# A first phase that multiplies the scaled x and leaves norm and shift until the sums are read

## The chip, the cores and the metric

The kernel runs on one core of one Trainium2 chip. The metric is the device time in microseconds (us) of one execution. TensorE (PE in the profile) multiplies matrices; VectorE (DVE), ScalarE (ACT) and GpSimd (POOL) do elementwise work; SyncE (SP) issues most of the DMA transfers. Each engine works through its own list of instructions in order and waits on semaphores for the others.

## The reference

One layer of a hybrid backbone, with D = 2048 channels, 1024 latent tokens `x`, 256 context tokens `ctx`. Cut to what matters here:

```python
mod_x = silu(c) @ w_mod + b_mod               # 3 x 2048 values: shift, scale, gate
mod_c = silu(c_ctx) @ w_mod + b_mod
sh_x, sc_x, gt_x = split(mod_x, 3)
hx = rmsnorm(x, norm_g) * (1.0 + sc_x) + sh_x   # per token: x * rsqrt(mean(x*x) + eps) * norm_g
hc = rmsnorm(ctx, norm_g) * (1.0 + sc_c) + sh_c
px = split(hx @ w_in)                          # q/k, v, o, z, gates, two recurrent parts
pc = split(hc @ w_in)
# context scans of both head groups (mLSTM, RG-LRU), whose last states seed the latent scans
# latent scans, gated, concatenated to yx
x = x + gt_x * (yx @ w_out)
out = rmsnorm(x, final_g)
```

`hx @ w_in` is linear in `hx`. With r(t) the norm factor of token t, s(k) the scale of channel k and b(k) its shift, `hx[t,k] = x[t,k]*s(k)*r(t) + b(k)`, so the sum over k of `hx[t,k]*w[k,m]` equals `r(t) * sum(x[t,k]*s(k)*w[k,m]) + sum(b(k)*w[k,m])`.

## The kernel before

Channels lie on the 128 partitions, so `x` is held transposed in 16 tiles `xT[k]` of 128 channels by 1024 tokens; two neighbouring k make a pair j (8 pairs). A product in f32 is made as three products of operands split into a high and a low part: `hxh` and `hxl` for the activations, `whi` and `wlo` for the weights. Weights stream through a ring: SP loads `raw`, ACT writes `whi` (L227), DVE writes `wlo` (L228). The matmuls of a k run `whi*hxh`, `wlo*hxh`, `whi*hxl`.

**Phase A** (`phase_a`, L456 to L668). PE, DVE, ACT and SP work here in the order in which the code is written. SP first loads all 16 `xT` tiles (512 KB each), then 64 tiles `wm` of modulation weights (512 KB each, 8 per pair), with weight pieces `raw` and context tiles `cT` between them. The `wm` tiles share 32 slots (tag hx) with `xT`, `hxh` and `hxl`, and have two slots of their own; `wm_fill` issues as many loads as there are free slots. While x arrives, ACT squares it (L541), DVE adds pairs of squares (L542) and PE sums them over the channels with a matrix of ones (L544); ACT takes the root (L556) and DVE the reciprocal (L557), which gives `rxB`, the norm factor of each token on all partitions. For a pair j, `mv_group` (L504) multiplies the modulation weights, `mv_fin` transposes the result (L519) and finishes scale and shift in `ssa` (L522 to L531). `to_hx` then makes the two `hxh`/`hxl` tiles: x times scale times `rxB` on DVE (L569), plus shift on ACT (L570), the low part on DVE (L575). `main_a` (L626) runs 36 matmuls of 512 columns for each pair into six PSUM accumulators `acc`: three blocks of 128 output channels. The modulation of pair j+1 is interleaved with the products of pair j. In the last pairs the context tokens are normalised too (`ctx_pair`, L606, L607, L612).

At its end `raw_tile` (L708) copies the first two accumulators out on ACT; the two PSUM buffers that the next products need are taken until then.

**Phase B** runs the context tokens: products of the context heads (L685 to L687 and L1056 to L1058), the mLSTM gates and scans, then eight units for the recurrent part, each of which ends with a copy on ACT (L1090) and a DMA from POOL's queue (L1091). From here on a planner orders the work: a clock (`clk`) counts the time of the PE products issued so far, and small jobs (`clk.spawn`) are put into the other engines' lists when their planned time has come; a job's `yield 1.5` asks to go on 1.5 us later by that clock. `clk.until(f)` lets the planner run jobs until `f` holds, before the code that follows is written out. Temporary tiles come from pools of slots such as `CS`, nine tiles in phase B.

**`v_head0`** (L1294 to L1316) is the first product of the latent tokens after that: twice (g = 0, 1) 16 channel tiles with 12 matmuls of 272 columns each (L1302 to L1304), whose weights come from the ring in pieces of two k (128x544). It reads `hxh` and `hxl` of all 16 k. All other products of the latent tokens, the scans and the output projection follow.

The functions that the change touches:

Of the kernel before, what the change touches and what calls it, by code (L numbers as in the profile page):

```python
# [19 lines left out]
D = 2048  # L20
# [236 lines left out]
def tile_hymba(ctx: ExitStack, tc: tile.TileContext, x, x_t, ctx_t, vecs_t, w_mod_a, w_mod_g, b_mod, w_in,  # L257
# [76 lines left out]
    hch = hcs.tile([128, KT, CTX], F32R, name="hch")  # L334
    pap = lpool("pa", side="right")
# [75 lines left out]
    wm_n = {"next": 0, "keep": 5, "hx": -1}  # L411
# [6 lines left out]
    def wm_fill():  # L418

        while wm_n["next"] < 8 * KP:  # L420
            n = wm_n["next"]
            j = n // 8
            keep = wm_n["keep"] if j <= wm_n["hx"] + 1 else max(wm_n["keep"], 2)
            if live["pa"] < NWM:
                live["pa"] += 1
                t, where = pa.tile([128, 2, 512], F32, tag="wm", bufs=NWM, name=f"wm{n}"), "pa"
            elif live["hx"] < NHX - keep:
                t, where = hx_tile([128, 2, 512], F32, f"wm{n}"), "hx"
            else:
                return  # L430
# [3 lines left out]
            if n == 8:  # L434
                ring._dma()
            if n == 23:
# [19 lines left out]
    def phase_a():  # L456
# [4 lines left out]
        for k in range(KT):  # L461
            xT[k] = hx_tile([128, SEQ], F32, f"xT{k}")
            SP.dma_start(out=xT[k], in_=x_t[k])
        ring._dma()
        wm_n["keep"] = 4
        wm_fill()
        silP = pa.tile([128, KT, 32], F32, name="silP")
        POOL.memset(silP, 0.0)
        act(out=cc[:, 1, :], in_=silc, func=AF.Sigmoid)
        act(out=cc[:, 2, :], in_=cc[:, 0, :], func=AF.Sigmoid)  # L470
        DVE.tensor_tensor(out=silc, in0=silc, in1=cc[:, 1, :], op=MUL)
        DVE.tensor_tensor(out=silP[:, :, 1], in0=cc[:, 0, :], in1=cc[:, 2, :], op=MUL)
        DVE.tensor_copy(out=silP[:, :, 0], in_=silc)
# [19 lines left out]
        def mv_group(j, g):  # L493
# [19 lines left out]
        def mv_fin(j):  # L513
# [20 lines left out]
        nacc = [mx_tile() for _ in range(2)]  # L534
        rxt = pa.tile([128, 2, SEQ], F32, tag="xp", bufs=1, name="rxt")
        rxB, vt = rxt[:, 0, :], rxt[:, 1, :]
        for j in range(KP):
            sq = []
            for u in range(2):
                sq.append(hx_tile([128, SEQ], F32, f"sq{2 * j + u}"))  # L540
                act(out=sq[u], in_=xT[2 * j + u], func=AF.Square)  # L541
            DVE.tensor_tensor(out=sq[0], in0=sq[0], in1=sq[1], op=ADD)  # L542
            for hf in range(2):
                PE.matmul(out=nacc[hf], lhsT=ones, rhs=sq[0][:, 512 * hf:512 * hf + 512], start=(j == 0), stop=(j == KP - 1))  # L544
            del sq
            live["hx"] -= 2
        wm_n["keep"] = 0
        wm_fill()
        for g in range(4):
            mv_group(0, g)  # L550
            if g == 1:
                for _ in range(2):
                    ring._split()
                for hf in range(2):
                    o = rxB[:, 512 * hf:512 * hf + 512]
                    act(out=o, in_=nacc[hf], func=AF.Sqrt, scale=1.0 / D, bias=eps)  # L556
                    DVE.reciprocal(out=o, in_=o)  # L557
        nacc.clear()

        def to_hx(j):  # L560
# [19 lines left out]
            if g == 1:  # L580
# [1042 lines left out]
```

## Time and profile before

| | |
|---|---|
| median of 3 runs | 1865.52 us (1865.25 to 1867.12) |
| profiled execution | 1863.79 us, its span 1862.0 us |
| mean granted clock of TensorE | 0.996 of full speed |
| PE busy | 1801.4 us, 97% of the span |
| DVE busy | 898.1 us, 48% |
| ACT busy | 772.2 us, 41% |
| POOL busy | 284.8 us, 15% |

The span is the time between the first and the last instruction that the profile records, and the 1.8 us between it and the execution's own time lie around it. The shares are means over the whole span; a stage in which PE waits for another engine is found by cutting the span into stretches.

### The profile page before, as it was taken

How to read it: one execution, taken by the hardware profiler on the slowest of the kernel's cores; microseconds unless marked ns; L12 is line 12 of the kernel's file. 1: busy time of each engine (PE TensorE's matmuls, PEld its weight loads, DVE VectorE, ACT ScalarE, POOL GpSimd, SP SyncE). 2: the span in 40 equal slices, each digit the busy share in tenths (PEclk: the TensorE clock that was granted, in tenths of full speed). 3: DMA queues.
4: the chain of work that ended last, by engine and by line, in shares of the span. 5: the costliest groups of instructions: out<-in, count | busy, mean ns of one | idle time of the engine just before them, and what ended most of it. 6: DMA issues, size and time to landing. Idle time of an engine off the chain costs nothing.

```text
span 1862.0 us, 24089 instructions
## 1 busy us (share of the span) xinstructions
PE 1801.4 (97%) x9114; PEld 1478.5 (79%) x9114; DVE 898.1 (48%) x1625; ACT 772.2 (41%) x1190; POOL 284.8 (15%) x382
## 2 busy tenths in 40 slices
PE   6998999999999999999999999999999999999998
PEld 2557999788897878987798878777888877888786
DVE  5576553436434664255443443655555454334432
ACT  5446542346645522133312422576555542223322
POOL 0000010012001210012000210222212332222320
PEclk9999999999999999999999999999999999999999
DMA  9974674212132334224342214122222584436533
GB/s 383 398 261 149 172 201 112 68 48 73 57 98 56 106 101 131 73 78 106 101 132 84 61 45 137 28 91 67 64 71 71 191 288 155 135 125 238 168 120 119
DMA packets 229444, 240.22 MB, mean 129 GB/s; under 512 B 25904, under 2 KB 184768, under 8 KB 229328
## 3 DMA queue, kind: packets, MB, share of 16 engines
q1 hardware_dynamic: 219360, 207.03, 36.5%
q0 software_dynamic: 4704, 16.78, 2.5%
q10 hardware_dynamic: 5264, 14.88, 2.0%
q8 instruction: 71, 1.16, 0.2%
q14 instruction: 45, 0.37, 0.1%
HBM read 210.78 MB, written 27.87 MB: 128 GB/s over the span
## 4 chain that ended last, share of the span: by engine, by line
PE 75%; DMA 9%; DVE 6%; issue 4%; ACT 4%; POOL 1%; SPq 0%; ACTq 0%; DVEq 0%; POOLq 0%
PE mm L1288 12%; PE mm L1285 12%; PE mm L1282 12%; PE mm L1325 2%; PE mm L1327 2%; PE mm L1328 2%; DMA wm<-in_w_mod_a_dram 2%; DMA raw<-in_w_out_dram 2%; PE mm L1470 2%; PE mx L1469 2%; PE mx L1471 2%; PE mx L1470 2%; PE mm L1471 2%; PE mm L1469 2%; DVE wlo L228 1%
## 5 line engine op out<-in xcount | busy, mean ns | idle before, releaser
L228 DVE TENSOR_TENSOR wlo<-raw,whi 128x512 fp32r<-128x512 f32 (+2 forms) x396 | 289.7, 741 | 577.1 <-ACT whi L227 576.1
L227 ACT ACTIVATE whi<-raw 128x512 fp32r<-128x512 f32 (+2 forms) x396 | 242.9, 624 | 563.8 <-PE mm L1285 249.3
L1282 PE MATMUL mm<-hxh,whi 128*128 128x512 f32 x1184 | 385.2, 406 | 0.3 <-DVE Gx L1314 0.3
L1288 PE MATMUL mm<-hxh,wlo 128*128 128x512 f32 x1184 | 373.2, 396 | 0.0
L1285 PE MATMUL mm<-hxl,whi 128*128 128x512 f32 x1184 | 372.7, 395 | 0.0
L1285 PEld LDWEIGHTS mm<-hxl,whi 128*128 128x128 f32 x1184 | 222.9, 188 | 52.9
L1288 PEld LDWEIGHTS mm<-hxh,wlo 128*128 128x128 f32 x1184 | 223.1, 188 | 51.7
L1282 PEld LDWEIGHTS mm<-hxh,whi 128*128 128x128 f32 x1184 | 221.2, 189 | 49.3 <-ACT s L1312 0.5
L1325 PE MATMUL mm<-whi,hxh 128*128 128x256 f32 x384 | 110.1, 287 | 0.3 <-DVE s L1363 0.2
L1327 PE MATMUL mm<-wlo,hxh 128*128 128x256 f32 x384 | 108.1, 281 | 0.0
L1328 PE MATMUL mm<-whi,hxl 128*128 128x256 f32 x384 | 107.4, 281 | 0.0
L1470 PE MATMUL mm<-wlo,hxh 128*128 128x512 f32 x224 | 88.7, 396 | 4.6 <-DVE wlo L228 4.6
L1469 PE MATMUL mm<-whi,hxh 128*128 128x512 f32 x224 | 88.3, 394 | 0.8 <-ACT whi L227 0.8
L1469 PE MATMUL mx<-whi,hxh 128*128 128x512 f32 x224 | 88.4, 395 | 0.0
L1471 PE MATMUL mx<-whi,hxl 128*128 128x512 f32 x224 | 88.1, 393 | 0.0
L1470 PE MATMUL mx<-wlo,hxh 128*128 128x512 f32 x224 | 88.1, 393 | 0.0
L1471 PE MATMUL mm<-whi,hxl 128*128 128x512 f32 x224 | 88.0, 393 | 0.0
L1039 DVE SCALAR_TENSOR_TENSOR r<-r,cols,r 128x256 f32<-128x256 f32 x120 | 60.1, 500 | 37.3 <-DMA r<-in_w_mod_g_dram 35.4
L1325 PEld LDWEIGHTS mm<-whi,hxh 128*128 128x128 f32 x384 | 72.4, 189 | 1.1 <-PE mx L1262 0.6
L1327 PEld LDWEIGHTS mm<-wlo,hxh 128*128 128x128 f32 x384 | 72.4, 188 | 0.3
L1328 PEld LDWEIGHTS mm<-whi,hxl 128*128 128x128 f32 x384 | 72.2, 189 | 0.0
L1507 POOL TENSOR_TENSOR res<-res,xpc 128x512 f32<-128x512 f32 x28 | 39.7, 1438 | 211.4 <-DMA raw<-in_w_out_dram 131.8
(324 smaller groups left out, 3055.1 us busy)
## 6 DMA issues: line engine op xcount, KB each, us to landing
raw<-in_w_in_dram SPq DMA_DIRECT2D x134, 512.0 KB
wm<-in_w_mod_a_dram SPq DMA_DIRECT2D x64, 512.0 KB
raw<-in_w_out_dram SPq DMA_DIRECT2D x64, 512.0 KB
r<-in_w_mod_g_dram SPq DMA_DIRECT2D x128, 128.0 KB
xT<-in_x_t_dram SPq DMA_DIRECT2D x16, 512.0 KB
NI<-niD SPq DMA_DIRECT2D x64, 128.0 KB
xpc<-in_x_dram SPq DMA_DIRECT2D x32, 256.0 KB
yD<-s ACTq DMA_DIRECT2D x15, 512.0 KB
```

The lines of the kernel that those rows point to most:

```text
L227: self.nc.scalar.activation(out=hi, in_=src, func=AF.Copy)
L228: self.nc.vector.tensor_tensor(out=lo, in0=src, in1=hi.bitcast(F32), op=SUB)
L1039: DVE.scalar_tensor_tensor(out=a, in0=t, scalar=silc[:, k:k + 1], in1=a, op0=MUL, op1=ADD)
L1282: PE.matmul(out=ps[:, ts], lhsT=hi, rhs=hxh[k][:, ts], start=(k == 0), stop=False)
L1285: PE.matmul(out=ps[:, ts], lhsT=hi, rhs=hxl[k][:, ts], start=False, stop=False)
L1288: PE.matmul(out=ps[:, ts], lhsT=lo, rhs=hxh[k][:, ts], start=False, stop=(k == KT - 1))
L1325: PE.matmul(out=o, lhsT=hxh[k][:, sl], rhs=hi, start=(k == 0 and tt % 2 == 0), stop=False, skip_group_check=True)
L1327: PE.matmul(out=o, lhsT=hxh[k][:, sl], rhs=lo, start=False, stop=False, skip_group_check=True)
L1328: PE.matmul(out=o, lhsT=hxl[k][:, sl], rhs=hi, start=False, stop=(k == KT - 1), skip_group_check=True)
L1469: PE.matmul(out=pst[jt], lhsT=hxh[j][:, sl], rhs=hi, start=(j == 0), stop=False)
L1470: PE.matmul(out=pst[jt], lhsT=hxh[j][:, sl], rhs=lo, start=False, stop=False)
L1471: PE.matmul(out=pst[jt], lhsT=hxl[j][:, sl], rhs=hi, start=False, stop=(j == KT - 1))
```

## The change

Phase A multiplies `x*scale` alone. The norm factor and the shift no longer stand in its operands, and so `x` need not all be there before the first product. The parts:

- SP loads eight `wm` tiles first, then `xT` two tiles at a time between the groups of eight `wm`, so that x and modulation weights of a pair arrive together. The rule for free slots in `wm_fill` is new; the last `xT` tile takes one of the two `wm` slots.
- `to_ux` takes the place of `to_hx`: ACT writes `hxh` straight from `xT` (Copy with scale, L569), ACT squares `xT` (L571, L573), POOL adds the square into `rxB` (L574, 128x1024, for 15 of the 16 k), DVE writes `hxl` (L577). The squares of all k but the first pass through one tile, `vt`.
- `x_norm` (L582 to L592), two matmuls with ones, two roots and two reciprocals, stands between the products of the last two k.
- `shift_sum` (L594 to L596): 32 DVE instructions of 128x384 sum the weights times shift into `wacc`; PE sums `wacc` over the channels at the end, DVE copies the result to `wb` (L695).
- `raw_tile` and `gate_tile` multiply the accumulators by `rxB` as they read them and add `wb`.
- Since later products need the full `hx`, a job `to_h` turns the tiles over in phase B: 64 blocks of 128x256, four for each k, each with two instructions on POOL (L875, L876), one on ACT (L878) and one on DVE (L879). The code waits for its end before `v_head0`.

```diff
 def wm_fill():
         while wm_n["next"] < 8 * KP:
             n = wm_n["next"]
             j = n // 8
-            keep = wm_n["keep"] if j <= wm_n["hx"] + 1 else max(wm_n["keep"], 2)
+            ahead = j - 1 - wm_n["hx"]
+            free = NHX - live["hx"] - (2 * ahead + 1 if ahead > 0 else 0)
+            if j and wm_n["x"] <= 2 * j + 1:
...
+                x_load()
+                continue
             if live["pa"] < NWM:
...
-            elif live["hx"] < NHX - keep:
+            elif free >= 1:
...
-            if n == 8:
+            if n == 7:
                 ring._dma()
+                x_load()
+                x_load()
...
+        wacc = pa.tile([128, 384], F32, name="wacc")
...
-        def to_hx(j):
+        def to_ux(j):
             for k in (2 * j, 2 * j + 1):
-                sh = ssa[:, k, 2:3]
+                sx = ssa[:, k, 0:1]
                 for ts in hs:
-                    DVE.scalar_tensor_tensor(out=vt[:, ts], in0=xT[k][:, ts], scalar=ssa[:, k, 0:1], in1=rxB[:, ts], op0=MUL, op1=MUL)
-                    act(out=hxh[k][:, ts], in_=vt[:, ts], func=AF.Identity, bias=sh)
+                    act(out=hxh[k][:, ts], in_=xT[k][:, ts], func=AF.Copy, scale=sx)
+                if k == 0:
+                    act(out=rxB, in_=xT[k], func=AF.Square)
+                else:
+                    act(out=vt, in_=xT[k], func=AF.Square)
+                    POOL.tensor_tensor(out=rxB, in0=rxB, in1=vt, op=ADD)
                 for ts in hs:
-                    DVE.scalar_tensor_tensor(out=hxl[k][:, ts], in0=vt[:, ts], scalar=sh, in1=hxh[k][:, ts].bitcast(F32),
-                                             op0=ADD, op1=SUB)
+                    DVE.scalar_tensor_tensor(out=hxl[k][:, ts], in0=xT[k][:, ts], scalar=sx, in1=hxh[k][:, ts].bitcast(F32),
+                                             op0=MUL, op1=SUB)
...
+        def x_norm():
+            ps = [mx_tile() for _ in range(2)]
+            for hf in range(2):
+                PE.matmul(out=ps[hf], lhsT=ones, rhs=rxB[:, 512 * hf:512 * hf + 512], start=True, stop=True)
+            for hf in range(2):
+                o = rxB[:, 512 * hf:512 * hf + 512]
+                act(out=o, in_=ps[hf], func=AF.Sqrt, scale=1.0 / D, bias=eps)
+                DVE.reciprocal(out=o, in_=o)
+
+        def shift_sum(k, w):
+            DVE.scalar_tensor_tensor(out=wacc, in0=w.bitcast(F32), scalar=ssa[:, k, 2:3], in1=wacc, op0=MUL, op1=ADD)
...
         def raw_tile(n, m):
             for hf in range(2):
-                act(out=j2r(st)[:, halves[hf], :], in_=jv(acc[m][hf]), func=AF.Copy)
+                DVE.tensor_tensor(out=j2r(st)[:, halves[hf], :], in0=jv(acc[m][hf]), in1=jv(rxB[:, 512 * hf:512 * hf + 512]), op=MUL)
             acc[m] = None
+            act(out=st, in_=st, func=AF.Identity, bias=wb[m])
...
+    def to_h():
+        for k in range(KT):
+            sh = b1sc[:, k:k + 1]
+            for q in range(4):
+                ts = slice(256 * q, 256 * q + 256)
+                hi = hxh[k][:, ts].bitcast(F32)
+                v = yield from CS.get()
+                v = v[:, 0:256]
+                POOL.tensor_tensor(out=v, in0=hi, in1=hxl[k][:, ts].bitcast(F32), op=ADD)
+                POOL.tensor_tensor(out=v, in0=v, in1=rxB[:, ts], op=MUL)
+                yield 1.5
+                act(out=hxh[k][:, ts], in_=v, func=AF.Identity, bias=sh)
+                DVE.scalar_tensor_tensor(out=hxl[k][:, ts], in0=v, scalar=sh, in1=hi, op0=ADD, op1=SUB)
+                CS.free()
+                yield 1.2
+        cflag["h"] = True
...
+    clk.spawn(to_h(), 10.0, P['hx'])
...
+    clk.until(lambda: "h" in cflag)
     for h in range(NH):
         if h == 0:
             v_head0()
```

Three places in the lists of the engines follow. The first is the end of phase A on DVE, from the modulation of the last pair to the first split of context weights behind it. Before:

```order
L569 SCALAR_TENSOR_TENSOR rxt<-xT_148,ssa,rxt 128x512 x2
L575 SCALAR_TENSOR_TENSOR hxl_1125<-rxt,ssa,hxh_1120 128x512 x2
L569 SCALAR_TENSOR_TENSOR rxt<-xT_150,ssa,rxt 128x512 x2
L575 SCALAR_TENSOR_TENSOR hxl_1133<-rxt,ssa,hxh_1128 128x512 x2
L228 TENSOR_TENSOR wlo_1154<-raw_1037,whi_1153 128x544
L606 SCALAR_TENSOR_TENSOR rxt<-cT_389,ssa,rcB 128x256 x2
L612 SCALAR_TENSOR_TENSOR hcl_1173<-rxt,ssa,hch 128x256 x2
L606 SCALAR_TENSOR_TENSOR rxt<-cT_391,ssa,rcB 128x256 x2
L612 SCALAR_TENSOR_TENSOR hcl_1186<-rxt,ssa,hch 128x256 x2
L228 TENSOR_TENSOR wlo_1190<-raw_1037,whi_1189 128x544
```

The changed kernel, from the low parts of the last pair (`hxl`) on; `vt` at L623 is the context scratch, which has the name of the squares' tile:

```order
L577 SCALAR_TENSOR_TENSOR hxl_1099<-xT_948,ssa,hxh_1094 128x512 x2
L577 SCALAR_TENSOR_TENSOR hxl_1107<-xT_950,ssa,hxh_1102 128x512 x2
L596 SCALAR_TENSOR_TENSOR wacc<-whi_940,ssa,wacc 128x384
L596 SCALAR_TENSOR_TENSOR wacc<-wlo_941,ssa,wacc 128x384
L228 TENSOR_TENSOR wlo_1130<-raw_1006,whi_1129 128x544
L596 SCALAR_TENSOR_TENSOR wacc<-whi_1009,ssa,wacc 128x384
L623 SCALAR_TENSOR_TENSOR vt<-cT_341,ssa,rcB 128x256 x2
L629 SCALAR_TENSOR_TENSOR hcl_1150<-vt,ssa,hch 128x256 x2
L596 SCALAR_TENSOR_TENSOR wacc<-wlo_1010,ssa,wacc 128x384
L623 SCALAR_TENSOR_TENSOR vt<-cT_343,ssa,rcB 128x256 x2
L629 SCALAR_TENSOR_TENSOR hcl_1164<-vt,ssa,hch 128x256 x2
L592 RECIPROCAL rxB<-rxB 128x512 x2
```

The two reciprocals of the norm and part of the shift sums now stand in this list behind the context pairs; two more shift sums, the copy of `wb` and the two reads of accumulators at L739 follow behind them.

The second place is POOL around the last DMA of the recurrent units (`xrcD`). Before:

```order
L1091 DMA xrcD<-c_2862 128x256
L1315 MEMSET s_3109 128x4
L811 MEMSET gxms 64x8
L995 MEMSET cwb 128x512
L745 MEMSET r_3807 128x1
L746 MEMSET r_3807 128x2
L739 TENSOR_SCALAR r_3861<-r_3807,cols 128x256
```

The changed kernel, from the last two such DMAs on:

```order
L1144 DMA xrcD<-c_2915 128x256
L875 TENSOR_TENSOR c_2999<-hxh_603,hxl_608 128x256
L875 TENSOR_TENSOR c_3004<-hxh_611,hxl_616 128x256
L1144 DMA xrcD<-c_2996 128x256
L876 TENSOR_TENSOR c_2999<-c_2999,rxB 128x256
L876 TENSOR_TENSOR c_3004<-c_3004,rxB 128x256
L875 TENSOR_TENSOR c_3009<-hxh_611,hxl_616 128x256
L875 TENSOR_TENSOR c_3014<-hxh_611,hxl_616 128x256
L876 TENSOR_TENSOR c_3009<-c_3009,rxB 128x256
L876 TENSOR_TENSOR c_3014<-c_3014,rxB 128x256
```

Behind the last `xrcD` stand the second instructions of two blocks of `to_h` (`c_2999`, `c_3004`) and then both instructions of 35 more blocks: 72 instructions of 128x256, from the last block of one k (`hxh_603`, which is k = 6) through k = 15.

The third place is ACT around the weight pieces of `v_head0` (L227, 128x544, two k each). Before, behind the copy of the last recurrent unit:

```order
L1090 ACTIVATE c_2862<-mm_2791 128x256
L227 ACTIVATE whi_2895<-raw_2773 128x544
L227 ACTIVATE whi_2926<-raw_2812 128x544
L227 ACTIVATE whi_2954<-raw_2812 128x544
L227 ACTIVATE whi_2985<-raw_2847 128x544
L227 ACTIVATE whi_3013<-raw_2847 128x544
```

The changed kernel, at the end of `to_h`; `hxh_1102` is the tile of k = 15:

```order
L878 ACTIVATE hxh_1094<-c_3159,b1sc 128x256
L878 ACTIVATE hxh_1102<-c_3164,b1sc 128x256
L878 ACTIVATE hxh_1102<-c_3169,b1sc 128x256
L878 ACTIVATE hxh_1102<-c_3174,b1sc 128x256
L878 ACTIVATE hxh_1102<-c_3179,b1sc 128x256
L227 ACTIVATE whi_3273<-raw_2941 128x544
L227 ACTIVATE whi_3304<-raw_2979 128x544
L227 ACTIVATE whi_3332<-raw_2979 128x544
```

The piece for k = 10 and 11 (`whi_3273`) now stands behind the last block of `to_h`, the piece for k = 8 and 9 behind the third block of k = 12, and the piece for k = 6 and 7 behind the third block of k = 7; DVE has its low parts in the same places.

## Rows read from the trace of the kernel before

**Rows 1.** Busy time by stretch: stretch, its length, engines with counts, PEclk, DMA, GB/s

```profile
0.00:41.27 41.27, 26.11 (x77) 9.05 (x77) 23.84 (x48) 24.38 (x29) 2.44 (x12) 1.00 0.98 380
41.27:138.40 97.13, 95.32 (x489) 51.62 (x490) 64.86 (x135) 39.19 (x68) 0.00 (x0) 1.00 0.91 334
138.40:150.50 12.10, 10.86 (x47) 8.46 (x45) 10.31 (x19) 7.50 (x12) 0.00 (x0) 1.00 0.13 35
150.50:283.00 132.50, 126.45 (x1010) 123.12 (x1011) 73.75 (x152) 70.46 (x122) 8.24 (x28) 1.00 0.67 187
283.00:307.70 24.70, 24.38 (x195) 24.06 (x193) 7.89 (x16) 6.43 (x11) 3.27 (x11) 1.00 0.48 122
307.70:1862.00 1554.30, 1518.25 (x7300) 1262.16 (x7300) 717.50 (x1259) 624.23 (x949) 270.83 (x331) 1.00 0.35 105
```

**Rows 2.** Chain of waits, first 165 us: start, length, what

```profile
6.86 9.81 DMA xT<-in_x_t_dram
...
78.40 0.44 PE mx L519 x4
...
91.92 0.44 PE mx L519 x4
...
112.92 6.92 DMA wm<-in_w_mod_a_dram
...
127.61 4.78 DMA wm<-in_w_mod_a_dram
...
150.50 0.39 PE mm L685
```

**Rows 3.** Groups by line, first 150 us: busy us, mean ns of one

```profile
L570 ACT ACTIVATE hxh<-rxt,ssa 128x512 fp32r<-128x512 f32 x32 | 22.2, 724 | 30.5 <-DVE rxt L569 28.0 <-DMA raw<-in_w_in_dram 2.4
L541 ACT ACTIVATE sq<-xT 128x1024 f32<-128x1024 f32 x16 | 15.8, 1046 | 2.5 <-PE mx L544 2.3 <-DVE sq L542 0.2
L228 DVE TENSOR_TENSOR wlo<-raw,whi 128x384 fp32r<-128x384 f32 x16 | 8.8, 554 | 14.9 <-ACT whi L227 14.9
L606 DVE SCALAR_TENSOR_TENSOR rxt<-cT,ssa,rcB 128x256 f32<-128x256 f32 x16 | 7.0, 479 | 0.0
L557 DVE RECIPROCAL rxt<-rxt 128x512 f32<-128x512 f32 x2 | 6.6, 3322 | 1.2 <-ACT rxt L556 1.2
L708 ACT ACTIVATE stx<-mm 128x512 f32<-128x512 f32 x2 | 1.9, 1048 | 0.0
```

**Rows 4.** POOL's groups by line and shape, whole span

```profile
L936 POOL TENSOR_TENSOR s<-s,s 128x1024 f32<-128x1024 f32 x16 | 38.5, 2405 | 125.6 <-ACT s L934 125.6
...
L1188 POOL TENSOR_TENSOR QI<-s,NI 128x128 f32<-128x128 f32 x64 | 33.2, 519 | 23.0 <-DVE s L1136 22.9
...
L968 POOL TENSOR_TENSOR s<-s,s 128x1024 f32<-128x1024 f32 x8 | 25.2, 3153 | 111.7 <-DVE s L958 111.7
L936 POOL TENSOR_TENSOR r<-r,r 128x256 f32<-128x256 f32 x16 | 11.9, 746 | 80.0 <-ACT r L934 65.7 <-DVE wlo L228 11.4 <-DMA raw<-in_w_in_dram 2.9
```

**Rows 5.** Timeline at 405 us: start, length, engine, line

```profile
405.42 0.69 DVE L228 TENSOR_TENSOR wlo<-raw,whi 128x512 fp32r<-128x512 f32 x1 [0.17 <-ACT whi L227]
...
405.56 0.86 POOL L1184 TENSOR_TENSOR D<-NI,msk 128x128 f32<-128x128 f32 x1 [5.03 <-DMA NI<-niD]
...
406.39 0.46 POOL L1188 TENSOR_TENSOR QI<-s,NI 128x128 f32<-128x128 f32 x1
```

**Rows 6.** Timeline at POOL's last unit DMA

```profile
284.32 0.54 POOL L1091 DMA_DIRECT2D xrcD<-c  x1 [5.19 <-ACT c L1090]
```

**Rows 7.** Timeline of ACT behind the last unit's copy

```profile
286.39 0.66 ACT L227 ACTIVATE whi<-raw 128x544 fp32r<-128x544 f32 x1 [2.36 <-PE mm L1304]
289.40 0.66 ACT L227 ACTIVATE whi<-raw 128x544 fp32r<-128x544 f32 x1 [2.35 <-PE mm L1304]
```

**Rows 8.** Timeline of PE at both ends of `v_head0`'s first half

```profile
283.01 0.29 PE L1302 MATMUL mm<-whi,hxh 128*128 128x272 f32 x1
...
307.08 0.29 PE L1304 MATMUL mm<-whi,hxl 128*128 128x272 f32 x1
```

**Rows 9.** Busy time by stretch where the granted clock falls, columns as before

```profile
350.00:354.00 4.00, 4.00 (x13) 2.94 (x14) 1.06 (x1) 1.16 (x2) 0.00 (x0) 0.57 0.10 13
```

More of the change, by code (lines that the diff above doesn't have):

```diff
@@ L334, in tile_hymba @@
     hch = hcs.tile([128, KT, CTX], F32R, name="hch")
+    rxB = hcs.tile([128, SEQ], F32, name="rxB")
     pap = lpool("pa", side="right")
@@ L410, in tile_hymba @@
     wm_t = {}
-    wm_n = {"next": 0, "keep": 5, "hx": -1}
+    wm_n = {"next": 0, "x": 0, "hx": -1}
     def hx_tile(shape, dtype, name):
@@ L433, in wm_fill, with x_load @@
             wm_t[n] = (t, where)
[L434 removed]
+            if n == 7:
                 ring._dma()
[L436 removed]
+                x_load()
+                x_load()
+            if n == 15:
+                ring._dma()
+            if n == 31:
                 for jc in range(KP):
                     load_ctx(jc)
+    def x_load():
+        k = wm_n["x"]
+        wm_n["x"] += 1
+        if k == KT - 1:
+            live["pa"] += 1
+            xT[k] = pa.tile([128, SEQ], F32, tag="wm", bufs=NWM, name=f"xT{k}")
+        else:
+            xT[k] = hx_tile([128, SEQ], F32, f"xT{k}")
+        SP.dma_start(out=xT[k], in_=x_t[k])
     def load_ctx(j):
@@ L460, in phase_a @@
         ncp = [hx_tile([128, SEQ], F32, "ncp")]
[L461 to L465, printed above, removed]
         wm_fill()
-        silP = pa.tile([128, KT, 32], F32, name="silP")
+        silP = pa.tile([128, 2 * KT + 32], F32, name="silP")
+        silV = silP[:, 0:2 * KT].rearrange("p (k s) -> p k s", s=2)
+        wacc = pa.tile([128, 384], F32, name="wacc")
         POOL.memset(silP, 0.0)
+        POOL.memset(wacc, 0.0)
         act(out=cc[:, 1, :], in_=silc, func=AF.Sigmoid)
@@ L531, in mv_fin @@
             DVE.tensor_tensor(out=ssa[:, ks, 2:4], in0=ssa[:, ks, 2:4], in1=two(cols[:, cSH + 2 * j:cSH + 2 * j + 2]), op=ADD)
[L534 to L548, printed above, removed]
+            DVE.tensor_copy(out=b1sc[:, ks], in_=ssa[:, ks, 2])
+        vt = pa.tile([128, SEQ], F32, tag="xp", bufs=1, name="vt")
         for g in range(4):
@@ L553, in phase_a @@
                     ring._split()
[L554 to L558, printed above, removed]
-        def to_hx(j):
+        def to_ux(j):
             if j >= KP:
@@ L603, in ctx_pair @@
             ks = (2 * j, 2 * j + 1)
-            fv = [vt[:, CTX * u:CTX * u + CTX] for u in range(2)]
+            o = 2 * CTX * (j % 2)
+            fv = [(ncp[0] if ncp else vt)[:, o + CTX * u:o + CTX * u + CTX] for u in range(2)]
             for k in ks:
@@ L660, in phase_a @@
                         ctx_norm(4 * j - 5)
+                    if j == KP - 2:
+                        ncp.clear()
+                        live["hx"] -= 1
                     mv_fin(j + 1)
-                    to_hx(j + 1)
+                    to_ux(j + 1)
+                    for w in (hi, lo):
+                        shift_sum(k, w[:, 0, :])
                     some(15)
-            if j == 4:
-                ncp.clear()
-                live["hx"] -= 1
-                wm_fill()
+        ps = mx_tile()
+        for m in range(3):
+            PE.matmul(out=ps[:, 4 * m:4 * m + 4], lhsT=wacc[:, cs_of[m]], rhs=ones[:, 0:4], start=True, stop=True)
+        wb = pa.tile([128, 12], F32, name="wb")
+        DVE.tensor_copy(out=wb, in_=ps[:, 0:12])
+        acc.append([wb[:, 4 * m:4 * m + 1] for m in range(3)])
         return acc
@@ L713, in gate_tile @@
             if hf == 0:
-                acc.append(pa.tile([128, 2, SEQ], F32, tag="xp", bufs=1, name="stz"))
-            stz = acc[3]
-            sg = stz[:, 0, 512 * hf:512 * hf + 512]
-            act(out=sg, in_=acc[1][hf], func=AF.Sigmoid)
-            DVE.tensor_tensor(out=j2r(stz[:, 1, :])[:, halves[hf], :], in0=jv(acc[1][hf]), in1=jv(sg), op=MUL)
+                acc.append(pa.tile([128, SEQ], F32, tag="xp", bufs=1, name="stg"))
+                acc.append(pa.tile([128, SEQ], F32, tag="wm", bufs=NWM, name="stz"))
+            stg, stz = acc[3:5]
+            zt, sg = stg[:, 0:512], stg[:, 512:1024]
+            DVE.tensor_tensor(out=zt, in0=acc[1][hf], in1=rxB[:, 512 * hf:512 * hf + 512], op=MUL)
+            act(out=sg, in_=zt, func=AF.Sigmoid, bias=wb[1])
+            DVE.scalar_tensor_tensor(out=j2r(stz)[:, halves[hf], :], in0=jv(zt), scalar=wb[1], in1=jv(sg), op0=ADD, op1=MUL)
             if hf:
-                ACT.dma_start(out=pre[1], in_=stz[:, 1, :])
+                ACT.dma_start(out=pre[1], in_=stz)
                 acc[1] = None
```

22 lines of the change are left out of this document (14 added, 8 removed).

## The prediction

> **What bounds the kernel now.** I read the page first: PE is busy for 97% of the span, so a gain can only come from a stretch in which PE has little to do, and a loss from any stretch in which the change makes PE wait. Cutting the span by stage [rows 1] shows where. Up to 41.27 us PE is busy for 26.11 us with the norm's sums and the first modulation weights, and the first real product starts at its end; DMA moves 380 GB/s there. Up to 138.40 PE is busy for 95.32 of 97.13 us. The next stretch, to 150.50, is the end of phase A, and from there to 283.00 the context runs. The first half of `v_head0` takes 283.01 to about 307.1, the start and near the end of it [rows 8]; behind it PE has 1518 of 1554 us.
>
> Then the chain of waits [rows 2]. It begins with DMA (x until 16.7), then follows PE pair by pair: the transposes of successive pairs stand at 78.40 and 91.92, 13.5 us apart, the 36 matmuls of one pair and the modulation work of the next. For the last pairs a `wm` transfer is in the chain again, 6.92 and 4.78 us from issue to landing, because a slot has to come free first. The context's first product is at 150.50, 12.1 us behind the ready scale of the last pair (138.40).
>
> **The change in phase A.** *The start.* The first product then needs eight `wm`, one weight piece, four x tiles and two more `wm` of the next pair: about 15 transfers of 0.52 MB, 7.9 MB, which at 380 GB/s [rows 1] take 20.7 us after the first 2 us, so products start near 23 instead of 41.3: 18 us earlier. What follows is no longer PE's pace. A pair now needs 8 `wm`, 2 x and a piece, 5.8 MB, 15 us at 380 GB/s, against 13.5 us of PE [rows 2]; so DMA sets the pace and the lead shrinks to about 10 us at the last pair but one.
>
> *The last pair.* I expect most of the lead lost here. By the lists, the loads of x15 and of the last pair's `wm` wait for slots: `wm` 58 for the matmul of 57, 61 for that of 59, 63 for that of 61. With the landing times of the two `wm` transfers in the chain (4.78 and 6.92 us [rows 2]) and about 1 us of matmuls behind each, three such steps make 18 to 24 us behind the first quarter (near 114); with the transposes and the scale behind them I take 135 for the ready scale, against 138.4. Its bounds: 126 if the stream stays unbroken (80 transfers of 0.52 MB and some 6 MB of pieces and context, 48 MB at 380 GB/s), 139 if the loads come late throughout.
>
> *The tail.* Before, the context starts 12.1 us behind the scale. Now the norm hangs on the last x tile's square, and the squares pass through one tile, `vt`. Behind the scale stand, each waiting for the one before: two `hxh` halves on ACT (2 x 0.72) and a square (1.05) [rows 3], an add of 128x1024 on POOL (2.41 [rows 4]), the last square (1.05; it may not write `vt` before the add has read it), the last add (2.41): 8.4 us. Beside the adds DVE makes low parts from two inputs in SBUF, for which I add 1.7 us (below), and some 0.9 us for the hand-overs: 11.0. Only now is `vt` free for the context pairs' scratch: eight DVE instructions at 0.48 [rows 3], 3.8 us; the root (0.2 us not hidden); two reciprocals at 3.32, 6.6; one split of 0.7; two shift sums of 128x384 at 0.55, 1.1; the sum of `wacc` and its copy, 1.2 (two engine hand-overs); two reads of accumulators at the 1.05 us that ACT needs for a half [rows 3], 2.1. Together 15.7, so the context starts 26.7 us behind the scale. At 135 + 26.7 = 161.7 it is **11.2 us** later than 150.50. Before, the same reciprocals lay under the wait for `wm`. Bounds: 126 + 25 = 151 to 139 + 28 = 167, or 0 to +16.5.
>
> PE has little to do for the 20 us ahead of that point. The stretch at 350 us [rows 9] has a granted clock of 0.57, near the lower level (1.2 GHz), for 4 us, with PE busy throughout: a loss of 4 x 0.43 = 1.7 us. I add **1.7** for each long stop of PE. In that row the fall comes without an idle stretch ahead of it, so it carries the price and not the cause. The Trainium skill (TensorE: Matmul & The Clock Gate, Part 1: The HAM clock gate) says that an idle array falls back to 1.2 GHz and is given the full clock again only after working for a while; by that both stops pay once, and without it the sum is 3.4 us less. No row here shows a fall after idling.
>
> **The change in phase B.** `to_h` issues 64 x 2 POOL, 64 ACT and 64 DVE instructions. Those on ACT and DVE lie in the context stage, where each has some 60 us free of 132.5 [rows 1]; I put them at nothing there, with 0 to 6 us as the bound if they delay weight splits. POOL decides. Its list holds the `xrcD` DMAs between the blocks, and each waits for the copy of its recurrent unit: the last one issues at 284.32, for 0.54 [rows 6], behind a wait of 5.19 us, so POOL does not run past that point before it. With T0 = 283.01 the start of `v_head0` [rows 8], POOL is free at T0 + 1.85. The order shows 72 of its instructions still behind. The nearest row is the same shape and operation kind, 128x256 at 0.746 [rows 4]: 72 x 0.746 = 53.7 us.
>
> Beside them runs DVE's L879, two inputs in SBUF. The timeline at 405 us [rows 5] shows what this does: a 128x128 instruction on POOL takes 0.86 us while DVE's two-input split (0.69) overlaps 0.55 of it, and the next, alone, 0.46; so 0.40 is lost in 0.55 of overlap, about 75%. One L879 per block at 0.48 (L606 is the same form [rows 3]) costs POOL 0.36, 36 times 13.0 us. The Trainium skill (GPSIMD Engine Reference, 8. Key points) has the rule: GpSimd shares its SBUF interfaces with VectorE and is hindered by DVE instructions with two SBUF inputs. The trace agrees by these two durations. Taking the row without the rule, as an accident of this one place, `to_h` would end 13 us earlier, which is a rival below.
>
> POOL ends at T0 + 1.85 + 53.7 + 13.0 = T0 + 68.6. Then L878 on ACT (0.45), and behind it the weight piece for k = 10, 11: split on ACT 0.66 [rows 7], low part 0.7; PE goes on at T0 + 70.4. PE has done k = 0 to 9 by then: up to k = 7 unhindered at T0 + 12, k = 8 and 9 once the piece behind the third block of k = 12 is through, some 45 us behind T0. Three pieces are left, 3.0 us each by the distance of successive pieces [rows 7], 9.0, and 1.7 for the clock: T0 + 81.1, against T0 + 24.1. That is **57.0 us** lost. Nothing gives it back, since everything that follows needs this output or PE, which had 2% free there. Of the stop itself weight loads profit, but PE did not wait for these.
>
> Bounds for POOL's part: 128x1024 at 2.41 is 0.60 for each 256 columns, and 128x128 at 0.46 alone [rows 4, 5]: a 128x256 can hardly be under 0.6, 72 x 0.6 = 43.2, less 10.5; from L968, 3.15 for 128x1024, 0.79 a quarter and 0.15 for the start, 0.94, 72 x 0.94 = 67.7, more 14.
>
> **Sum.** 11.2 + 1.7 + 57.0 = 69.9 us. Against the profiled execution of 1863.8 (span 1862.0 and 1.8 around it) it gives 1933.7; the median lies 1.7 higher, 1865.5, and gives 1935.4. I say **1935**.
>
> **The rivals.**
> 1. *No contention.* POOL holds 0.746 beside DVE. The tail is 1.7 shorter, `to_h` 13: 1935 - 15 = 1920. For it: 0.746 is a mean over instructions that ran beside DVE's ordinary work already. Against: the row at 405 us.
> 2. *POOL slower still*, by the rate of L968 (0.94), or DVE's other instructions hindering it too: 1935 + 14 = 1949.
> 3. *`to_h` hidden, the tail shows.* If POOL did a block within the 24 us of the first half, only phase A and one clock term count: 1865.5 + 11.2 + 1.7, about 1878. It needs 36 blocks in 24 us, 0.33 us an instruction; POOL takes 0.46 for half the columns. Against it speak all of POOL's rows.
> 4. *The other side.* The DMA stream stays unbroken: x arrives with its weights, nothing waits for a slot, and the last scale is ready at 126, 12 us before now. The price of the tail, 14.6 us more than now, is then nearly paid, and the waits of the early context stage for weights shrink (6 of 132.5 us are idle [rows 1]): 126 + 25 = 151, less up to 6, so 145 to 151 against 150.5. If `to_h` is hidden as in rival 3, the time is 1860 to 1866. The point from which it decides is the same 0.33 us on POOL; with POOL as its rows show, an unbroken stream alone gives 1925.
>
> **How the numbers follow.** 0.2% is 3.7 us; differences below it can't be told from no change here. My forecast with its own spread (1926 to 1943) has 0.50; rival 1 0.22, rival 2 0.13, rival 3 0.07, rival 4 0.05, anything else 0.03. Adding both phase A bounds (-11, +5) to the outer values of rivals 1 and 2 gives 1909 to 1954; beyond it on the lower side lie rivals 3 and 4 (0.12), so the range of 8 in 10 is 1898 to 1955. Faster: 0.03 of rival 4. Same: 0.02. Slower: 0.95.
>
> **What would show it.** In the profile after: first product of phase A near 23 us (start); a `wm` transfer as the chain's cause in the last pair, scale at 126 to 139; the two reciprocals behind the adds of POOL and ahead of the first context product near 162 (tail); POOL without a pause behind its last `xrcD`, 66 to 70 us long, its 128x256 instructions alternating between about 0.75 and 1.1 (contention); PE idle twice in `v_head0`, at k = 8 and k = 10, ended by a weight split whose engine was held by `to_h`. The forecast is wrong if POOL's blocks lie well ahead of `v_head0` in time, if its instructions take under 0.5 us, or if PE finds other work during the stop.

## The result, and the profile after

The changed kernel takes 1955.92 us (median of 4 runs, 1954.85 to 1957.21), against 1865.38 for the kernel before on the same chip: a ratio of 1.048, interval 1.0465 to 1.0495. The forecast was 1935 with a range to 1955; the direction holds, and the measured time lies 0.9 us beyond the upper end. The profiled execution took 1956.38 us, its span 1954.6.

The span cut at the marks that answer to [rows 1] (columns as there: stretch, its length, engines with counts, PEclk, DMA, GB/s): first product, last pair's scale, first context product, `v_head0`, its second half.

```profile
0.00:24.90 24.90, 11.58 (x44) 2.17 (x44) 8.71 (x39) 9.08 (x14) 4.37 (x14) 0.85 0.95 365
24.90:147.30 122.40, 105.00 (x494) 56.60 (x493) 82.69 (x138) 49.92 (x80) 31.58 (x13) 0.91 0.86 322
147.30:174.11 26.81, 15.62 (x57) 11.37 (x55) 23.06 (x26) 8.69 (x15) 5.16 (x2) 0.81 0.08 21
174.11:325.90 151.79, 137.41 (x1011) 132.01 (x1012) 112.04 (x183) 81.17 (x149) 56.60 (x84) 0.93 0.57 160
325.90:399.39 73.49, 32.52 (x195) 30.88 (x193) 40.46 (x52) 24.69 (x48) 60.87 (x83) 0.67 0.16 41
399.39:1954.60 1555.21, 1519.49 (x7300) 1262.92 (x7300) 717.94 (x1261) 624.42 (x949) 272.80 (x331) 1.00 0.35 105
```

Against [rows 1]: the context starts 23.6 us later (174.11 for 150.50), its stage is 19.3 longer (151.8 for 132.5), the first half of `v_head0` 48.8 longer (73.5 for 24.7), the rest 0.9. Together 92.6, which is the difference of the spans (1954.6 less 1862.0). The stage in which I had put the conversion at nothing (bound 6) took a fifth of the loss.

The groups of DVE in the first 174 us (busy us, mean ns of one) show the first sign of why.

```profile
L577 DVE SCALAR_TENSOR_TENSOR hxl<-xT,ssa,hxh 128x512 fp32r<-128x512 f32 x32 | 34.0, 1101 | 10.3 <-ACT hxh L569 10.3
L596 DVE SCALAR_TENSOR_TENSOR wacc<-wlo,ssa,wacc 128x384 f32<-128x384 f32 x16 | 23.8, 1488 | 0.4
L596 DVE SCALAR_TENSOR_TENSOR wacc<-whi,ssa,wacc 128x384 f32<-128x384 f32 x16 | 9.7, 604 | 0.0
```

Two shift sums of the same shape and form differ by a factor of 2.5: the one that falls beside POOL's add takes 1488 ns, the other 604. The extreme case stands behind the last `xrcD`. DVE's timeline there, then POOL's (start, length, engine, line):

```profile
326.66 0.73 DVE L228 TENSOR_TENSOR wlo<-raw,whi 128x544 fp32r<-128x544 f32 x1 [0.71 <-ACT whi L227]
329.11 10.82 DVE L879 SCALAR_TENSOR_TENSOR hxl<-c,b1sc,hxh 128x256 fp32r<-128x256 f32 x4 [1.72 <-ACT hxh L878]
```

```profile
327.77 1.44 POOL L876 TENSOR_TENSOR c<-c,rxB 128x256 f32<-128x256 f32 x2
329.17 1.43 POOL L875 TENSOR_TENSOR c<-hxh,hxl 128x256 f32<-128x256 f32 x2
...
336.12 1.40 POOL L876 TENSOR_TENSOR c<-c,rxB 128x256 f32<-128x256 f32 x2
337.88 1.76 POOL L875 TENSOR_TENSOR c<-hxh,hxl 128x256 f32<-128x256 f32 x2 [0.36 <-DVE hxl L879]
```

POOL runs at 0.70 us an instruction, as if alone, while DVE's first L879 (0.48 alone) does not get through: it begins at 329.11 and ends only when POOL itself pauses, at 337.5, for want of a `CS` tile that this very instruction still reads. The chain of waits gives this one instruction 8.71 us.

The theory for the experiments: POOL and DVE share a path into SBUF that one of them holds for a whole instruction; a DVE instruction with two inputs in SBUF waits for it, and POOL's back-to-back instructions pass it on to each other. The first half agrees with the Trainium skill (SBUF — State Buffer, Who interferes with whom), which calls the shared port pair an exclusive lock, held for the whole instruction, that a two-input DVE instruction contends for with GpSimd's reads. That POOL's next instruction takes the lock ahead of the DVE instruction that waits is read from the rows above alone. The rivals: proportional slowing, as in the prediction; slots and transfers in phase A; the added work itself.

### The profile page after: what moved, and what is told of

It reads as the page before. It is cut to its first block, busy times and chain, and to the rows that moved or that the text cites. A ratio compares the mean times of both kernels' runs of the same rounds, so it can differ in the third digit from the quotient of the medians.

```text
span 1954.6 us, 24332 instructions
## 1 busy us (share of the span) xinstructions
PE 1821.6 (93%) x9092; PEld 1495.9 (77%) x9092; DVE 984.9 (50%) x1696; ACT 798.0 (41%) x1252; POOL 431.4 (22%) x526
## 4 chain that ended last, share of the span: by engine, by line
PE 67%; DVE 10%; DMA 10%; ACT 5%; issue 4%; POOL 4%; SPq 0%; ACTq 0%; DVEq 0%; POOLq 0%
PE mm L1341 11%; PE mm L1338 11%; PE mm L1335 11%; DMA wm<-in_w_mod_a_dram 3%; DVE wlo L228 3%; DMA raw<-in_w_out_dram 3%; PE mm L1378 2%; PE mm L1380 2%; PE mm L1381 2%; PE mm L1524 2%; PE mx L1523 2%; PE mx L1525 2%; PE mx L1524 2%; PE mm L1525 2%; PE mm L1523 2%
## 5 line engine op out<-in xcount | busy, mean ns | idle before, releaser
L228 DVE TENSOR_TENSOR wlo<-raw,whi 128x512 fp32r<-128x512 f32 (+2 forms) x396 | 301.0, 772 | 566.1 <-ACT whi L227 559.5
L227 ACT ACTIVATE whi<-raw 128x512 fp32r<-128x512 f32 (+2 forms) x396 | 242.5, 624 | 577.1 <-PE mm L1338 246.4
L1237 POOL TENSOR_TENSOR D<-NI,msk 128x128 f32<-128x128 f32 x64 | 31.5, 491 | 215.3 <-DMA NI<-niD 131.2
```

Of the source, the lines that this page charges most:

```text
L227: self.nc.scalar.activation(out=hi, in_=src, func=AF.Copy)
L228: self.nc.vector.tensor_tensor(out=lo, in0=src, in1=hi.bitcast(F32), op=SUB)
```

## Experiments

The tables of stages below come from the profiled execution of each kernel, at the same marks: start of the context, its stage, first half of `v_head0`.

### Without to_h

```diff
-    clk.spawn(to_h(), 10.0, P['hx'])
-    clk.until(lambda: "h" in cflag)
```

> The job to_h and the wait for it are left out (the latent products then run on x times scale, so the output is not the layer's). Theory (the shared path between POOL and DVE is held by one of them for a whole instruction, and POOL's back-to-back adds and products in to_h keep DVE's two-input splits out): phase A stays as in the changed kernel (context starts near 174, +23.6), the context stage falls back from 151.8 to 133-137 us, the first half of v_head0 from 72.4 to 24-25; time 1890 to 1895. Rival (the context stage is longer because it starts with a low clock and late weights): it stays near 148-152 us, time 1905 to 1910.

Measured: 172.7, 137.4, 24.6; 1895.5 us, ratio 1.0141 (1.0118 to 1.0164). The theory's numbers, stage and time 0.4 and 0.5 us over their upper ends. So 14.4 us of the context stage's 19.3 come from `to_h`. The other 4.9 go with a clock of 0.96 in place of 1.00: PE's matmuls are busy for 130.76 us where [rows 1] have 126.45, 4.3 more, and 0.6 is idle time. The row of this run:

```profile
172.70:310.10 137.40, 130.76 (x1011) 127.31 (x1012) 76.97 (x156) 71.08 (x122) 8.08 (x28) 0.96 0.62 177
```

### Without to_h and without POOL's adds

```diff
-                    POOL.tensor_tensor(out=rxB, in0=rxB, in1=vt, op=ADD)
```

> As the run without to_h, and the 15 POOL adds of squares are left out too (the norm is then that of one channel tile). Theory (POOL's adds lock DVE's low parts and shift sums out, 15 us of DVE time in phase A, and the norm waits for the last add): the scale of the last pair is ready at 138-142 instead of 147, the tail behind it is 22-23 instead of 26.8, the context starts at 160-165. Rival (transfers and slots alone set the pace of phase A): the scale stays at 146-148, only the tail is shorter, context at 169-171.

Measured: the last transpose starts at 139.9 for 144.6 in the run above, the context starts at 164.5 for 172.7; 1884.96 us, ratio 1.0083 (1.0066 to 1.01). The low parts and the shift sums have their short lengths again (a line is gone, so L577 and L596 are L576 and L595 here):

```profile
L576 DVE SCALAR_TENSOR_TENSOR hxl<-xT,ssa,hxh 128x512 fp32r<-128x512 f32 x32 | 22.6, 749 | 10.3 <-ACT hxh L569 10.3
L595 DVE SCALAR_TENSOR_TENSOR wacc<-wlo,ssa,wacc 128x384 f32<-128x384 f32 x16 | 9.9, 616 | 0.4
```

The adds cost 4.7 us ahead of the scale and 3.5 in the tail. But the scale is still not early: the transposes of the last pair but one come at 115.5 and the last ones 24 us later, so the adds are 4.7 of the 12 us by which I missed the scale. Since the run takes away the adds themselves, it does not separate their lock on DVE from ACT's wait for `vt`, except in the tail, where the chain below runs through the held DVE instructions.

### to_h without its DVE instruction

```diff
-                DVE.scalar_tensor_tensor(out=hxl[k][:, ts], in0=v, scalar=sh, in1=hi, op0=ADD, op1=SUB)
```

> to_h without its DVE instruction (the low parts stay those of x times scale). Theory of the exclusive path: POOL runs without a stop at 0.70 us an instruction, 72 of them 50.4 us, so the first half of v_head0 takes 64-65 instead of 72.4; the weight splits are still kept out by POOL, so the context stage stays well above 132.5, at 142-150. Rival (DVE and POOL slow each other in proportion to the overlap, L879 being the disturber): context back at 133-136, v_head0 at 66-68.

Measured: 173.5, 146.7, 68.1; 1948.06 us, ratio 1.0414 (1.0394 to 1.0434). The context stage went as the theory had it (the rival's 133 to 136 is out), `v_head0` did not, its 68.1 lies by the rival's 66 to 68: I had left out that the weight splits are two-input instructions as well. DVE's timeline, then PE's:

```profile
327.43 45.02 DVE L228 TENSOR_TENSOR wlo<-raw,whi 128x544 fp32r<-128x544 f32 x2 [5.71 <-ACT whi L227]
```

```profile
371.33 0.59 PE L1355 MATMUL mm<-wlo,hxh 128*128 128x272 f32 x1 [41.66 <-DVE wlo L228]
```

Two splits of 0.72 us take 45.0 us, while POOL runs from 322.1 to 371.8 without a pause; PE stands for 41.7 us. L879 was not the disturber but another victim, and by blocking POOL through the tile it reads it had even opened a gap in which DVE got on. Most of the 41.7 us PE would have lost without the lock as well, since ACT splits the piece for k = 10 and 11 only behind the last block of `to_h`, as the lists above have it:

```profile
372.32 0.64 ACT L227 ACTIVATE whi<-raw 128x544 fp32r<-128x544 f32 x1
```

### POOL's time in writes only

```diff
-                POOL.tensor_tensor(out=v, in0=hi, in1=hxl[k][:, ts].bitcast(F32), op=ADD)
-                POOL.tensor_tensor(out=v, in0=v, in1=rxB[:, ts], op=MUL)
+                for _ in range(5):
+                    POOL.memset(v, 1.0)
```

> In to_h the two POOL instructions that read (add, product) are replaced by five memsets of the same 128x256 tile, which only write (values of hx are then constant plus shift); POOL is as busy, and the order on ACT, DVE and POOL around the recurrent units is about the same. Theory (it is POOL's reads that shut DVE's two-input instructions out): L879 at 0.48 and splits at 0.69 throughout, context 133-137 us, v_head0's first half still 60-75 us because POOL's list is as long; time 1930 to 1945. Rival (DVE is slow because of the added DVE and ACT work or its order, not because of POOL's reads): context 148-152 as before, time 1950-1956.

Measured: 173.7, 138.3, 51.8; 1923.12 us, ratio 1.0286 (1.0271 to 1.0301). DVE's groups from 174 to 320 us (the context stage, and here 8 us more), in this run and then in the changed kernel:

```profile
L228 DVE TENSOR_TENSOR wlo<-raw,whi 128x512 fp32r<-128x512 f32 x72 | 49.4, 689 | 24.5 <-ACT whi L227 23.9
L879 DVE SCALAR_TENSOR_TENSOR hxl<-c,b1sc,hxh 128x256 fp32r<-128x256 f32 x31 | 14.4, 482 | 9.8 <-ACT hxh L878 9.8
```

```profile
L228 DVE TENSOR_TENSOR wlo<-raw,whi 128x512 fp32r<-128x512 f32 x69 | 58.5, 858 | 20.5 <-ACT whi L227 20.0
L879 DVE SCALAR_TENSOR_TENSOR hxl<-c,b1sc,hxh 128x256 fp32r<-128x256 f32 x26 | 18.1, 716 | 1.4 <-ACT hxh L878 1.4
```

With ACT, DVE and the order much the same, POOL's reading in place of writing costs the context stage 13.5 us (151.8 less 138.3); the conversion's own ACT and DVE work costs 0.9 (138.3 less 137.4). POOL is not quite as busy: 46.6 us of the stage for 56.6, and what the difference is worth was not measured; but with it at work for these 46.6 us no DVE group is longer than without `to_h` (690 and 482 ns there for the splits and for L775, a two-input instruction of L879's shape). `v_head0` (51.8 for 60 to 75) and the time (7 us under the forecast) came out lower since five memsets took 1.3 us a block, less than the two reads.

### to_h issued sooner

```diff
-                yield 1.5
+                yield 0.9
...
-                yield 1.2
+                yield 0.6
```

> The planner may issue a block of to_h every 1.5 us of its clock instead of every 2.7, so that only 28 POOL instructions instead of 72 stand behind the last xrcD DMA. Theory (the stop in v_head0 is POOL's list behind that DMA; the exclusive path costs the context stage about 0.5 us for each block that lies in it): context stage 158-166 instead of 151.8, first half of v_head0 38-44 instead of 73, time 1928 to 1938. Rival (POOL's total work is what counts, wherever it is issued): what v_head0 gains the context stage loses, time 1950 to 1958.

Measured: 172.3, 165.3, 43.2; 1936.67 us, ratio 1.038 (1.0352 to 1.0407). Both stages go as the theory had it. 30 of POOL's instructions stand behind the last `xrcD`, for 72; the 21 blocks that moved out of `v_head0` save 30.3 us there and cost 13.5 in the context stage, 0.6 each.

### The adds of squares on DVE

```diff
-                    POOL.tensor_tensor(out=rxB, in0=rxB, in1=vt, op=ADD)
+                    DVE.tensor_tensor(out=rxB, in0=rxB, in1=vt, op=ADD)
```

> The 15 adds of squares run on DVE instead of POOL (same result; DVE has 15 more instructions of 128x1024, some 18 us). Theory (POOL's adds keep DVE out for longer than they would cost it, some 24 us): last scale at 142-146, context start at 168-172 instead of 174, time 1949 to 1954. Rival (DVE is the slowest engine of phase A by its own work): context start at 178-190, time 1960 to 1972.

Measured: 173.7, 150.6, 73.2; 1953.44 us, ratio 1.0474 (1.0443 to 1.0505). Neither: the start of the context did not move by more than 0.5 us. POOL's lock on DVE and DVE's own adds cost phase A the same, so the add has no cheap place here.

### The norm behind the first context products

```diff
-                    if j == KP - 1:
-                        x_norm()
...
+            act(out=j2r(st0)[:, halves[hf], :], in_=jv(acc[0][hf]), func=AF.Copy)
...
+            if k == 1:
+                wb.extend(finish())
+                raw_late()
```

(`finish` holds `x_norm`, the sum of `wacc` and the copy to `wb`; `raw_late` applies norm and shift to the copy.)

> The norm and the sum of the shifts are moved behind the second k of the first context product, and the first accumulator is copied out by ACT without norm (norm and shift are applied to the copy later), so that the context's products wait for neither; same result. Theory (the tail of 26.8-28 us is the chain of last add, roots, reciprocals and reads of accumulators): the context starts 12-17 us behind the last scale; the reciprocals then hold DVE's splits up for 4-7 us in the context stage; time 1942 to 1950. Rival (the tail is due to the context pairs and splits, as it was before): context start stays within 4 us of 174, time 1952 to 1958.

Measured: 163.1, 163.3, 72.2; 1954.61 us, ratio 1.0479 (1.0444 to 1.0514). The context starts 17.8 us behind the last transposes, 11.0 us earlier than in the changed kernel, and its stage is 11.5 us longer: all of it is given back. PE's waits between 163 and 215 us (us in total, times, longest) and DVE's timeline say where:

```profile
PE mm L716 <- ACT whi L227: 9.2, 3, 6.5
```

```profile
168.68 6.56 DVE L592 RECIPROCAL rxB<-rxB 128x512 f32<-128x512 f32 x2 [4.39 <-ACT rxB L591]
...
175.19 2.05 DVE L779 TENSOR_TENSOR stx<-stx,rxB 128x512 f32<-128x512 f32 x2
179.51 1.36 DVE L228 TENSOR_TENSOR wlo<-raw,whi 128x544 fp32r<-128x544 f32 x2 [2.28 <-ACT whi L227]
```

The reciprocals and the reads behind them still stand in DVE's list, now ahead of the weight splits; between 164.3 and 179.5 DVE makes no split, and ACT, whose next split stands behind the shift of the copy, waits for it as well. I had priced the reciprocals alone.

### The last pair with half of its weights

```diff
-        while wm_n["next"] < 8 * KP:
+        while wm_n["next"] < 8 * KP - 4:
```

> The modulation of the last pair uses four of its eight wm tiles; the other four are not loaded (the scale and shift of the last two k are then wrong). Theory (the last pair's loads each wait for a slot that the tile before frees): three waits of 3.5 to 5.5 us go, the last scale comes 10-14 us earlier, the context starts at 161-165, time 1942 to 1946. Rival (bandwidth or DVE sets the end of phase A): 2 MB less is 5 us at 400 GB/s, or nothing: context at 169-174, time 1951 to 1956.

Measured: last transposes 140.3 for 146.0, context at 168.3; 1946.54 us, ratio 1.0425 (1.0392 to 1.0457). A gain of 5.7, the rival's size, so the last four loads were worth 5 us and not 10 to 14. The context start and the time fall between the two forecasts. Nor is it bandwidth, the rival's reason: SP's issues in the changed kernel (start, time from the first issue's wait to the last issue) have their waits spread over the last two pairs, 21.2 us of them for slots that PE's L523 frees,

```profile
99.68 12.39 SPq L439 DMA_DIRECT2D wm<-in_w_mod_a_dram  x3
...
117.32 9.45 SPq L439 DMA_DIRECT2D wm<-in_w_mod_a_dram  x3
...
127.88 12.61 SPq L439 DMA_DIRECT2D wm<-in_w_mod_a_dram  x5
```

and DMA moves 188 GB/s from 121.5 to 147.3 where it had 394 to 402 until 104.5. Which slots would have to be freed earlier was not tried.

### x loaded again in place of POOL's work

```diff
+            SP.dma_start(out=v, in_=x_t[k][:, 256 * q:256 * q + 256])
...
+            DVE.scalar_tensor_tensor(out=v, in0=v, scalar=cols[:, cSC + k:cSC + k + 1], in1=rxB[:, ts], op0=MUL, op1=MUL)
```

> No POOL work in phase A or to_h: the squares are added on DVE, and to_h loads x from memory again in blocks of 128x256 (three ahead) and makes hx with two DVE instructions and one ACT instruction for each block; the planner may issue a block every 2.0 us. Same result. Theory (POOL's reads were the cost of the conversion): the context starts near 174 as in the run with DVE adds, context stage 140-148, first half of v_head0 25-32, time 1897 to 1912, still slower than before because phase A stays 22 us longer. Rival (the conversion itself costs that much on any engine): 1930 to 1955.

Measured: 174.7, 145.2, 39.7; 1919.74 us, ratio 1.028 (1.0263 to 1.0296). The cheapest full version tried, 36 us under the changed kernel; the context stage is as forecast, `v_head0` 8 us over, since 28 of the 64 blocks were left for it and DVE's list of them stood in front of a split:

```profile
PE mm L1368 <- DVE wlo L228: 10.5, 1, 10.5
```

### POOL's instructions alone in the kernel before

```diff
+                POOL.tensor_tensor(out=v, in0=hxh[k][:, ts].bitcast(F32), in1=hxl[k][:, ts].bitcast(F32), op=ADD)
+                POOL.tensor_tensor(out=v, in0=v, in1=v, op=MUL)
```

> The kernel before, with to_h's POOL instructions added at the same pace and nothing else: 64 times an add of hxh and hxl and a product, of 128x256, into a scratch tile that nobody reads; same result as before. Theory (POOL's reads lock DVE's two-input instructions out, in a back-to-back run until POOL's list pauses): context stage 142-150 instead of 132.5, first half of v_head0 60-72 instead of 24.7 although nothing depends on POOL, a DVE split of tens of us in the trace, time 1910 to 1925. Rival (to_h costs time through the waits for its results): no change, 1864 to 1872.

Measured: 152.0, 138.9, 55.7; 1908.7 us, ratio 1.0221 (1.0205 to 1.0238). 41 us for work that nobody reads, and splits in the context stage at 844 ns where they are 690 in the kernel before and in the changed kernel without `to_h`. The stage is under the forecast, and the split of tens of us did not come: POOL runs from 292.8 to 340.6 without a pause, but the five splits beside it take 1.09 to 1.19 us each, and POOL's instruction beside each becomes longer too. One of them, and POOL's rows there (a pair of L841 takes 1.17 us where no split is beside it):

```profile
303.96 1.17 DVE L228 TENSOR_TENSOR wlo<-raw,whi 128x544 fp32r<-128x544 f32 x1 [1.85 <-ACT whi L227]
```

```profile
303.11 1.42 POOL L840 TENSOR_TENSOR c<-hxh,hxl 128x256 f32<-128x256 f32 x2
304.50 1.66 POOL L841 TENSOR_TENSOR c<-c 128x256 f32<-128x256 f32 x2
```

So POOL's running without a pause is not enough to keep DVE out. One difference from `to_h` is the product, which here reads one tile twice; whether that lets DVE in was not tested. The stop in `v_head0` is of another kind: PE waits once, 31.3 us at the end of the first half, for `Gx`, a small sum that DVE makes of the finished product. DVE's timeline:

```profile
340.79 0.30 DVE L823 COPY gxms<-m 4x1 f32<-4x1 f32 x2 [32.64 <-POOL gxms L811]
```

DVE waits in order for a small memset (`gxms`) that stands behind POOL's run, and `Gx` and its splits wait behind that copy. So this run shows that the load on POOL alone costs the context stage 6.4 us; some 31 of the 41 us are the order of the lists and not the lock, and a DVE instruction held for tens of us is shown by the run without L879 alone.

## Why the prediction was right or wrong

The forecast loss was 69.9 us, the measured one 92.6. The start of the context came 12.4 us later than forecast and the context stage cost 19.3 that the sum did not have, while `v_head0` cost 8.2 less. That the time ends so near the range is luck in part: two terms were priced too low and one too high, and the upper end was built from a slower POOL (rival 2), which did not come.

- **Start of phase A**: right; the first product is at 24.9 (forecast near 23).
- **Pace and last scale**: wrong by 12 us. The step that failed is the lead of 10 us at the last pair but one: the transposes there come at 121.45, against 122 before. About 6 us of it go with POOL's adds (115.5 without them), beside which DVE's instructions are longer; a pair that took 20.7 us (transposes at 49.6 and 70.3) while DMA ran at 394 GB/s with the context tiles in the stream is the likely rest, not tested by itself. The last pair itself took 24 us, the upper end of the 18 to 24 of the prediction, but the picture of three waits for single slots was too simple.
- **Tail**: 26.8 us against 26.7 in the sum. Term by term the chain shows what was in it and what was not:

```profile
150.07 3.04 DVE hxl L577 x2
153.10 0.54 DVE wacc L596
153.67 2.60 DVE wacc L596
...
165.26 3.29 DVE rxB L592
...
172.96 1.02 DVE stx L739
```

  It does not run through POOL's adds, as I had it, but through the DVE instructions that these adds keep waiting (150.07 and 153.67):

```profile
149.50 2.39 POOL L574 TENSOR_TENSOR rxB<-rxB,vt 128x1024 f32<-128x1024 f32 x1 [17.57 <-ACT vt L573]
153.06 2.77 POOL L574 TENSOR_TENSOR rxB<-rxB,vt 128x1024 f32<-128x1024 f32 x1 [1.17 <-ACT vt L573]
```

  The sum is right, two of its terms are exchanged, and that they are of one size is luck.
- **Context stage**: wrong. The step "I put them at nothing there" counted the free time of ACT and DVE (60 of 132.5 us each), left POOL's effect on DVE's splits out, and bounded the whole at 6: 13.5 us are POOL's reads in place of writes, 0.9 the added work, 4.9 the lower clock that the stage starts with.
- **`v_head0`**: 48.8 against 57.0, with the mechanism right: POOL's 72 instructions behind the last `xrcD` end at 385.9, 60 us behind T0 (forecast 68.6). They cost 0.81 us each, not 0.93. The two stops of PE at k = 8 and 10 came as forecast, 19.6 and 14.7 us, ended by ACT's splits behind `to_h`. A third, of 5.8 us, came ahead of them, for the split that DVE had behind the held L879; it delays the time little, since PE had to stop for the next piece anyway.
- **The contention** is where the reading failed, and the rows were there. In [rows 5] POOL's 128x128 instruction starts at 405.56, DVE's split ends at 406.11 (405.42 + 0.69), and POOL ends at 406.42, 0.31 later. I read this as 75% lost while both ran; it fits an instruction that did most of its work once the other was nearly done, for 0.31 is less than the 0.46 of one alone. Read as a lock, the row says that whoever comes first wins; that DVE can lose beside an engine that does not pause, it does not say. Rival 2 named "DVE's other instructions" only as disturbers of POOL.
- **Clock**: the stop costs about what was priced (1.7). PE has little work for 36 us, and after it resumes runs at 0.52, near the lower level (1.2 GHz), for 5 us more, a loss of 2.4:

```profile
350.00:386.00 36.00, 6.17 (x24) 5.54 (x24) 14.65 (x23) 11.78 (x24) 35.92 (x48) 0.55 0.00 0
...
388.00:393.00 5.00, 5.00 (x23) 5.00 (x24) 1.22 (x4) 0.09 (x1) 0.00 (x0) 0.52 0.84 223
```

  That is the fall after idling that no row of before showed. What I missed is that it is also low in phase A, after PE's waits there (0.91 from 24.9 to 147.3), and that the context starts with it (0.69 from 174.1 to 180.0; the 4.9 us of the run without `to_h`).

Rivals 1, 3 and 4 are out: POOL's instructions took 0.81 us beside DVE, neither 0.746 nor 0.33, and an unbroken stream did not come about. Rival 2 is nearest in time (1949), but not by its 0.94 for an instruction of POOL. No version that was run is faster than the kernel before; the start that the change wins (16 us) is lost again before the context begins, in every version of the change.

## What to carry to other kernels

Work moved to an idle POOL is not free for DVE: if it reads SBUF, each two-input DVE instruction beside it may wait, in the worst run here for the end of POOL's whole list, so price it by DVE's list, and look for DVE instructions whose length differs between two places. When two overlapping instructions stretch, compare the end of one with the end of the other before you take a percentage. Work taken off the path of one wait still stands in an engine's in-order list: see what is queued behind it there.

## What the hardware showed that was not expected

- A DVE instruction of 0.72 us can be held for tens of us (two in 45.0) by POOL instructions of 0.70 in a row; POOL was not slowed by the waiting DVE. It need not be: beside the run of another pair of POOL instructions, in the last experiment, splits took 1.09 to 1.19 us and POOL gave way.
- POOL at work on memsets for 46.6 us of the stage left DVE's two-input instructions at 689 and 482 ns.
- Where POOL has once paused for a tile that DVE holds, the two alternate and POOL's mean rises from 0.70 to 0.81; without L879, and so without that pause, DVE did not finish a split from 330 to 371 us. What decides which engine gives way at the end of an instruction stays open.
